# Layer change with pinned norms, projection matmuls grouped by weight part, and attention's low parts by accumulating DMA

## The chip, the cores and the metric

One core of one Trainium2 chip runs one launch. The metric is the device time of that launch in microseconds; less is better. A profile is one further execution, taken with the hardware profiler.

## The reference, cut to what matters

Two blocks run one after the other on 512 tokens of width 1024 in fp32.

```python
def first_block(x, ...):                      # one layer, 16 meta tokens ahead of x
    proj = rmsnorm(h, g) @ w_in               # u, q, k, v, g_ssm, g_att
    y_ssm = s5_mixer(u, ...)                  # complex scan
    q, k = rmsnorm(q, qg) * scale, rmsnorm(k, kg)
    o = diff_attention(q, k, v, lam, slopes)  # 4 heads, two softmaxes each
    h = h + mixed @ w_o
    h = h + conv_glu_ffn(rmsnorm(h, g2), ...)

def second_block(x, ...):
    for l in range(2):
        proj = rms_norm(x, pre_norm_g[l]) @ w_in[l]   # a_*, b_*, c_*, d_*
        y = concat(conformer(a), hgrn2(b), ssd(c), mla(d)) @ w_out[l]
        x = x + rms_norm(y, post_norm_g[l])
```

The stretch between `@ w_out[0]` and the projections of layer 1 is the layer change: the norm of `y` needs all of `y`, and every projection of layer 1 needs the new `x`.

## The kernel before

**Matrix work.** Each fp32 operand is split into a high part (`xh`, `wh`, the value rounded by a copy to fp32r) and a low part (`xl`, `wl`, the value minus the high part), and each product is three matmuls a 128-row block: `wh·xh`, `wh·xl`, `wl·xh`. Activations lie feature by token in eight tiles `hT` (128x512); `xn` holds their eight pairs `xh`, `xl`.

**Weights.** `weights()` hands out tiles in one fixed order and has four fetched ahead. `_fetch` makes a pair of 128x1024 parts: a DMA of SP into `wr`, a copy of ACT into `wh` (L439), a copy of ACT of `-wh` into `wl` (L441), then a DMA issued by POOL that adds the same weights from memory into `wl` (L442). `wh` and `wl` have four buffers each, so a new pair's copies wait until TensorE has used up the pair four back.

**Buffers.** PSUM banks come from rings: `pj` has three, `sA` and `sB` two each, `so` one. SBUF work tiles ("units") are reused first in, first out.

**Order.** A scheduler of the framework sets each engine's order from the program's order and its own plan. `tc.high_priority` moves an instruction up, `tc.keep_in_program_order` (called `pin` in the diff) fixes it to its place among the pinned ones and its neighbours. Side work (attention, the conv, scans) runs as generators: each `pump()` in a projection takes one step (up to the next `yield`) of each of them.

**Attention.** `qk_norm` normalises one tile of q or k. `k_parts` makes, for each half of the 128 partitions, a tile `ks` with the high part on one half (ACT, L1032) and the low part on the other (POOL subtraction, L1033). `q_parts` makes two tiles `qq` of high parts on both halves (ACT, L1044, L1045) and one `ql` of low parts (POOL subtraction, L1046). `attention_head` uses them in the scores (L1174, L1175).

**Second block.** `fm` is a projection with features on partitions (one weight pair, 24 matmuls of 512 columns); `tm` is one with tokens on partitions: two weight pairs, two banks `p`, 96 matmuls of 256 columns (L1480 to L1482), first all 48 of one bank, then all 48 of the other. `b_f` and `b_q` feed the hgrn branch: `zr` scales them (DVE, L1603), `hgrn_decay` takes the sigmoids (ACT, L1632, L1633) and the decay (DVE, L1646, a scan at L1651), and its scores are at L345. The projection after them, `tm` of mla's keys and ssd's steps, is called kvm below; the next is `d_cq`. Six `tm` run in a layer, in two rows of three; ACT copies each bank out (L2249).

**Layer change.** `out2(n, w, hs)` is output tile n of `@ w_out[0]` for a half `hs` of the tokens (24 matmuls, L2335 to L2337), the copy to `os[n]` and the addition of its squares into `st` (`ns_add`, ACT L528 and DVE L529). Tiles 0 to 4 run whole, 5 to 7 by halves `ha`, `hb`. `ns_finish(st, half)` is the norm: a matmul that sums the squares (L537) and two ACT operations (`rsqrt`, L498, L499). `add` multiplies by it (DVE, L2351), adds into `hT` (L2353; every third on POOL), splits into `xh`, `xl` (ACT L487, DVE L488) and adds the squares of the new `hT` into `self.st`. `lead(half)` is the first three projections of layer 1 (`b_f0`, `b_f1`, `b_q0`) for a half, 72 matmuls (L2366, L2368, L2369) into two `pj` banks and `so`.

Of the kernel before, what the change touches and what calls it, by code (L numbers as in the profile page):

```python
# [312 lines left out]
class Build:  # L313
# [172 lines left out]
    def split_scale(self, src, scale, xh, xl):  # L486
        self.nc.scalar.activation(out=xh, in_=src, func=AF.Copy, scale=scale)  # L487
        self.nc.vector.scalar_tensor_tensor(out=xl, in0=src, scalar=scale, in1=xh.bitcast(F32), op0=ALU.mult, op1=ALU.subtract)  # L488

# [5 lines left out]
    def rsqrt(self, p, out, eps):  # L495
        nc = self.nc
        with self.tc.issue_after(self.lnexp):
            nc.scalar.activation(out=out, in_=p, func=AF.Ln, bias=eps)  # L498
            nc.scalar.activation(out=out, in_=out, func=AF.Exp, scale=-0.5)  # L499
# [60 lines left out]
    def split_g(self, xn, n, x, g, hs):  # L560
        xh, xl = xn[n]
        self.split_scale(x, g[:, n:n + 1], xh[:, hs], xl[:, hs])
# [897 lines left out]
    def fm(self, l, nm, i):  # L1460
        w = self.weights(("in2", (l, nm, i)))
        p = self.pj()
        self.mm3(p, w[0], w[1], 0, 128, 8, self.xn, slice(0, S), mid=True)
        return p

    def tm(self, l, nm, N=256):
        mm = self.nc.tensor.matmul
        ws = [self.weights(("in2", (l, nm, i))) for i in range(2)]
        for b in range(2):
            p = self.pj()  # L1470
            for u in range(2):
                if u:
                    self.pump()
                o = p[:, u * 256:u * 256 + N]
                sl = slice((b * 2 + u) * 128, (b * 2 + u) * 128 + 128)
                for k in range(8):
                    c = slice((k % 4) * 256, (k % 4) * 256 + N)
                    h, lo = ws[k // 4][0][:, c], ws[k // 4][1][:, c]
                    xh, xl = self.xn[k]
                    mm(out=o, lhsT=xh[:, sl], rhs=h, start=k == 0, stop=False)  # L1480
                    mm(out=o, lhsT=xh[:, sl], rhs=lo, start=False, stop=False)  # L1481
                    mm(out=o, lhsT=xl[:, sl], rhs=h, start=False, stop=k == 7)  # L1482
            yield b, p
# [731 lines left out]
    def layer(self, l):  # L2215
# [37 lines left out]
        q0 = zs.pop()  # L2253
        kf = []
# [5 lines left out]
        q1 = self.zr(self.fm(l, "b_q", 1))  # L2260
# [66 lines left out]
        def out2(n, w, hs):  # L2327
# [20 lines left out]
        def add(hs, r):  # L2348
            for n in range(8):
                o = os[n][:, hs]  # L2350
                V.tensor_tensor(out=o, in0=o, in1=r[:, hs], op=ALU.mult)  # L2351
                E = G if n % 3 == 0 else V
                E.tensor_tensor(out=x[n][:, hs], in0=x[n][:, hs], in1=o, op=ALU.add)  # L2353
                self.split_g(self.xn, n, x[n][:, hs], self.v("preg1"), hs)
# [3 lines left out]
        def lead(hs, wl):  # L2358
            mm = nc.tensor.matmul
            for a in range(2):  # L2360
                for k in range(8):
                    xh, xl = self.xn[k]
                    c = slice(k * 128, k * 128 + 128)
                    for w, p in zip(wl, self.lead):
                        if a == 0:
                            mm(out=p[:, hs], lhsT=w[0][:, c], rhs=xh[:, hs], start=k == 0, stop=False)  # L2366
                        else:
                            mm(out=p[:, hs], lhsT=w[0][:, c], rhs=xl[:, hs], start=False, stop=False)  # L2368
                            mm(out=p[:, hs], lhsT=w[1][:, c], rhs=xh[:, hs], start=False, stop=k == 7)  # L2369
# [122 lines left out]
```

## Time and profile before

| what | value |
| --- | --- |
| median of 3 runs | 1374.3 us (1372.24 to 1375.38) |
| profiled execution | 1374.76 us, span 1373.0 us |
| TensorE (PE) busy | 1329.0 us, 97% of the span |
| VectorE (DVE), ScalarE (ACT), GpSimd (POOL) busy | 787.3, 780.8, 449.1 us |
| granted TensorE clock, mean | 0.988 |

The span is the profile's first to last instruction; the execution's own time is 1.76 us longer. With TensorE at 97%, the 44 us in which it stands idle and the stretches with a lower granted clock are where time can be had without fewer matmuls, and the table does not say where they lie. The rows below do.

### The profile page before, as it was taken

How to read it: one execution, taken by the hardware profiler on the slowest of the kernel's cores; microseconds unless marked ns; L12 is line 12 of the kernel's file. 1: busy time of each engine (PE TensorE's matmuls, PEld its weight loads, DVE VectorE, ACT ScalarE, POOL GpSimd, SP SyncE). 2: the span in 40 equal slices, each digit the busy share in tenths (PEclk: the TensorE clock that was granted, in tenths of full speed). 3: DMA queues.
4: the chain of work that ended last, by engine and by line, in shares of the span. 5: the costliest groups of instructions: out<-in, count | busy, mean ns of one | idle time of the engine just before them, and what ended most of it. 6: DMA issues, size and time to landing. Idle time of an engine off the chain costs nothing.

```text
span 1373.0 us, 22963 instructions
## 1 busy us (share of the span) xinstructions
PE 1329.0 (97%) x8778; PEld 1193.8 (87%) x8778; DVE 787.3 (57%) x1951; ACT 780.8 (57%) x1218; POOL 449.1 (33%) x557
## 2 busy tenths in 40 slices
PE   8999999999999999999999999899999789899998
PEld 8988899999999988998898889789988788789986
DVE  8989775423524322332233385998732785998623
ACT  7556564654555444444444766765566666764653
POOL 4557632113332211222123443532212344522210
PEclk9999999999999999999999999999999889999999
DMA  8944566598888888888887966994477367894483
GB/s 281 239 96 108 120 128 139 123 222 184 187 194 185 186 187 188 187 189 185 197 175 150 227 132 148 192 191 88 99 164 191 90 133 167 178 202 92 94 182 92
DMA packets 76861, 223.49 MB, mean 163 GB/s; under 512 B 11216, under 2 KB 21968, under 8 KB 76752
## 3 DMA queue, kind: packets, MB, share of 16 engines
q0 software_dynamic: 32256, 106.53, 46.7%
q1 hardware_dynamic: 43488, 113.80, 25.4%
q10 hardware_dynamic: 1008, 1.70, 0.4%
q8 instruction: 69, 1.13, 0.3%
q14 instruction: 40, 0.33, 0.1%
HBM read 209.33 MB, written 4.72 MB: 156 GB/s over the span
## 4 chain that ended last, share of the span: by engine, by line
PE 80%; DVE 14%; ACT 2%; issue 2%; DMA 1%; POOL 1%; SPq 0%; DVEq 0%; ACTq 0%; POOLq 0%
PE pj L466 18%; PE pj L467 18%; PE pj L468 18%; PE pj L1480 3%; PE pj L1482 3%; PE pj L1481 3%; PE sB L492 2%; DVE cc L1508 2%; PE sB L2152 1%; PE so L2180 1%; PE pj L2335 1%; PE pj L2336 1%; PE pj L2337 1%; DVE hx L1680 1%; PE so L1212 1%
## 5 line engine op out<-in xcount | busy, mean ns | idle before, releaser
L466 PE MATMUL pj<-xh,wh 128*128 128x512 f32 (+4 forms) x1700 | 556.5, 328 | 4.4 <-ACT mk L2120 2.4
L467 PE MATMUL pj<-xl,wh 128*128 128x512 f32 (+4 forms) x1700 | 553.1, 326 | 0.0
L468 PE MATMUL pj<-xh,wl 128*128 128x512 f32 (+4 forms) x1700 | 551.3, 325 | 0.0
L439 ACT ACTIVATE wh<-wr 128x1024 fp32r<-128x1024 f32 (+2 forms) x197 | 203.7, 1035 | 324.4 <-PE pj L467 294.1
L442 POOL DMA_DIRECT2D wl<-in_wst x192 | 169.3, 882 | 555.2 <-ACT wl L441 525.9
L466 PEld LDWEIGHTS pj<-xh,wh 128*128 128x128 f32 x1700 | 320.7, 189 | 33.0 <-ACT mk L2120 2.9
L467 PEld LDWEIGHTS pj<-xl,wh 128*128 128x128 f32 x1700 | 320.6, 189 | 27.0 <-issue 0.9
L468 PEld LDWEIGHTS pj<-xh,wl 128*128 128x128 f32 x1700 | 320.7, 189 | 26.3
L441 ACT ACTIVATE wl<-wh 128x1024 fp32r<-128x1024 f32 (+2 forms) x192 | 198.9, 1036 | 3.0 <-PE pj L468 0.2
L1481 PE MATMUL pj<-wl,xh 128*128 128x256 f32 x384 | 112.1, 292 | 5.5 <-DMA wl<-in_wst 5.5
L1480 PE MATMUL pj<-wh,xh 128*128 128x256 f32 x384 | 111.9, 292 | 2.1 <-DVE u L1603 2.1
L1482 PE MATMUL pj<-wh,xl 128*128 128x256 f32 x384 | 111.0, 289 | 0.0
L1481 PEld LDWEIGHTS pj<-wl,xh 128*128 128x128 f32 x384 | 74.1, 193 | 7.5 <-DMA wl<-in_wst 5.7
L1480 PEld LDWEIGHTS pj<-wh,xh 128*128 128x128 f32 x384 | 73.9, 192 | 3.5 <-ACT hk L1633 2.2
L1482 PEld LDWEIGHTS pj<-wh,xl 128*128 128x128 f32 x384 | 74.1, 193 | 1.6 <-issue 1.4
L1508 DVE SCALAR_TENSOR_TENSOR cc<-u,aw,cc 128x511 f32<-128x511 f32 (+20 forms) x84 | 67.0, 804 | 0.9
L1404 DVE TENSOR_TENSOR hT<-hT,pj 128x512 f32<-128x512 f32 x24 | 16.4, 687 | 88.4 <-PE pj L468 88.4
L1383 DVE TENSOR_TENSOR u<-pj,nsR 128x258 f32<-128x258 f32 (+1 forms) x44 | 18.6, 425 | 75.6 <-PE pj L468 68.3
L1389 DVE TENSOR_TENSOR u<-u,pj 128x512 f32<-128x512 f32 x22 | 15.1, 688 | 64.5 <-PE pj L468 60.2
L529 POOL TENSOR_TENSOR nsA<-nsA,u 128x514 f32<-128x514 f32 (+3 forms) x23 | 29.3, 1274 | 38.3 <-ACT u L528 28.8
L488 DVE SCALAR_TENSOR_TENSOR xl<-hT,vec,xh 128x256 fp32r<-128x256 f32 (+3 forms) x40 | 27.5, 703 | 18.7 <-ACT xh L487 18.7
L1515 POOL DMA_DIRECT2D ce<-u x28 | 24.6, 918 | 40.3 <-ACT mq L2113 10.8
(629 smaller groups left out, 2353.6 us busy)
## 6 DMA issues: line engine op xcount, KB each, us to landing
wr<-in_wst SPq DMA_DIRECT2D x183, 512.0 KB, 4.1
wl<-in_wst POOLq DMA_DIRECT2D x180, 512.0 KB, 6.1
hT<-in_xT SPq DMA_DIRECT2D x16, 264.0 KB, 5.8
wr<-in_wst SPq DMA_DIRECT2D x8, 384.0 KB, 3.1
wl<-in_wst POOLq DMA_DIRECT2D x8, 384.0 KB, 5.1
wr<-in_wst SPq DMA_DIRECT2D x6, 256.0 KB, 5.6
UD<-us SPq DMA_DIRECT2D x4, 264.0 KB, 9.2
U<-UD SPq DMA_DIRECT2D x16, 66.0 KB, 4.6
```

The source lines that it names most:

```text
L439: nc.scalar.activation(out=h[:, c], in_=raw[:, c], func=AF.Copy)
L441: nc.scalar.activation(out=l[:, c], in_=h.bitcast(F32)[:, c], func=AF.Copy, scale=-1.0)
L442: nc.gpsimd.dma_start(out=l[:, c], in_=self.ap["wst"][i, :, c], accum_op=ALU.add)
L466: mm(out=out, lhsT=a, rhs=xh[:, sl], start=k == 0, stop=False)
L467: mm(out=out, lhsT=a, rhs=xl[:, sl], start=False, stop=False)
L468: mm(out=out, lhsT=b, rhs=xh[:, sl], start=False, stop=k == nk - 1)
L488: self.nc.vector.scalar_tensor_tensor(out=xl, in0=src, scalar=scale, in1=xh.bitcast(F32), op0=ALU.mult, op1=ALU.subtract)
L529: eng.tensor_tensor(out=st["A"][:, hs], in0=st["A"][:, hs], in1=s[:, hs], op=ALU.add)
L1480: mm(out=o, lhsT=xh[:, sl], rhs=h, start=k == 0, stop=False)
L1481: mm(out=o, lhsT=xh[:, sl], rhs=lo, start=False, stop=False)
L1482: mm(out=o, lhsT=xl[:, sl], rhs=h, start=False, stop=k == 7)
L1508: V.scalar_tensor_tensor(out=c[:, o:S], in0=th[:, :S - o], scalar=aw[:, i, 30 - o:31 - o], in1=c[:, o:S], op0=ALU.mult, op1=ALU.add)
```

## The change

There are four parts. (1) The low parts of k and q are made like those of the weights: ACT copies the negative into place, and a DMA issued by POOL adds the fp32 value. (2) Each attention head takes two more steps (two `yield`) before its first instruction. (3) `fm` and `tm` run the matmuls that need `wh` first, those with `wl` after them; `tm` has both banks open at once and goes weight pair by weight pair. (4) At the layer change the norm's matmul is put at a fixed place inside the following matrix work (`at`), the splits of the first half are pinned between the copies of `out2`, all additions into `hT` run on DVE, the squares come after all splits, the second `lead` runs output by output, and layer 1's `b_q1` comes earlier in the program.

```diff
-    def rsqrt(self, p, out, eps):
+    def rsqrt(self, p, out, eps, pin=None):
...
@@ k_parts
             nc.scalar.activation(out=t[a], in_=f[a], func=AF.Copy)
-            nc.gpsimd.tensor_tensor(out=t[b], in0=f[a], in1=t[a].bitcast(F32), op=ALU.subtract)
+            nc.scalar.activation(out=t[b], in_=f[a], func=AF.Copy, scale=-1.0)
+            nc.gpsimd.dma_start(out=t[b], in_=f[a], accum_op=ALU.add)
@@ q_parts
         lo = self.unit(F32R, "ql")
+        nc.scalar.activation(out=lo[:, :S], in_=f[:, NM:], func=AF.Copy, scale=-1.0)
+        nc.gpsimd.dma_start(out=lo[:, :S], in_=f[:, NM:], accum_op=ALU.add)
...
-            nc.gpsimd.tensor_tensor(out=lo[a, :S], in0=f[a, NM:], in1=t[a, :S].bitcast(F32), op=ALU.subtract)
@@ attention_head
             yield
+        yield
+        yield
@@ fm
-        self.mm3(p, w[0], w[1], 0, 128, 8, self.xn, slice(0, S), mid=True)
+        for k, (xh, xl) in enumerate(self.xn):
+            a = wh[:, k * 128:k * 128 + 128]
+            mm(out=p, lhsT=a, rhs=xh[:, :S], start=k == 0, stop=False)
+            mm(out=p, lhsT=a, rhs=xl[:, :S], start=False, stop=False)
+            if k == 5:
+                self.pump()
+        for k, (xh, xl) in enumerate(self.xn):
+            mm(out=p, lhsT=wl[:, k * 128:k * 128 + 128], rhs=xh[:, :S], start=False, stop=k == 7)
@@ tm
-        for b in range(2):
-            p = self.pj()
-            for u in range(2):
...
+        ps = [self.pj() for _ in range(2)]
+        for q in range(2):
+            for t in range(2):
+                for b, p in enumerate(ps):
+                    for u in range(2):
...
+                        for k in range(4):
+                            if t:
+                                mm(out=o, lhsT=xh[:, sl], rhs=ws[q][1][:, c], start=False, stop=q + u + k == 5)
+                            else:
+                                mm(out=o, lhsT=xh[:, sl], rhs=ws[q][0][:, c], start=q + u + k == 0, stop=False)
+                                mm(out=o, lhsT=xl[:, sl], rhs=ws[q][0][:, c], start=False, stop=False)
@@ layer
         q0 = zs.pop()
+        q1 = self.zr(self.fm(l, "b_q", 1)) if l else None
...
-        q1 = self.zr(self.fm(l, "b_q", 1))
+        if not l:
+            q1 = self.zr(self.fm(l, "b_q", 1))
@@ layer change: out2
             for q, k in enumerate(korder):
+                if q == 3 and at:
+                    at()
...
-            nc.scalar.activation(out=os[n][:, hs], in_=p, func=AF.Copy, scale=pg[:, n:n + 1])
-            self.ns_add(st, n, p, hs, V)
+            with self.tc.high_priority(offset=400 if hs.stop - hs.start < S else 0):
+                i = nc.scalar.activation(out=os[n][:, hs], in_=p, func=AF.Copy, scale=pg[:, n:n + 1])
+                if n > 5 and hs.start:
+                    pin(i)
+                self.ns_add(st, n, p, hs, V)
@@ layer change: lead
+            for k in range(8):
+                if k == 5 and at:
+                    at()
+                for i in range(3):
+                    m = part(0, k, i)
...
+            if at:
+                for a in (1, 2):
+                    for k in range(8):
+                        for i in range(3):
+                            part(a, k, i)
+            else:
+                for i in range(3):
+                    for a in (1, 2):
+                        for k in range(8):
+                            part(a, k, i)
+        def norm(hs):
+            def at():
+                p = self.sB()[:, :256]
+                pin(nc.tensor.matmul(out=p, lhsT=self.o1024, rhs=st["A"][:, hs], start=True, stop=True))
+                with self.tc.high_priority(offset=600):
+                    self.rsqrt(p, st["R"][:, hs], self.eps6, None)
+                add(hs, st["R"])
+            return at
@@ layer change: the calls
-        r = self.ns_finish(st, ha)
-        add(ha, r)
-        for n in range(5, 8):
-            out2(n, ws[n - 5], hb)
+        out2(5, ws[0], hb, norm(ha))
+        split(ha, range(4), pin)
+        out2(6, ws[1], hb)
+        split(ha, range(4, 8), pin)
+        out2(7, ws[2], hb)
...
-        lead(ha, ws)
-        r = self.ns_finish(st, hb)
-        add(hb, r)
+        lead(ha, ws, norm(hb))
+        split(hb, range(8))
+        square(ha)
+        square(hb)
```

**Place 1: ACT, the first half's splits.** Before, on ACT, the splits (L487, `xh`) of the first half stand in a row, each followed by the square of the same `hT` (L525, L528); the copy of the last `out2` tile (L2338, `po_10956`) comes after the first of them.

```order
L487 ACTIVATE xh_11159<-hT_4059,vec 128x256
L525 ACTIVATE nsA_11157<-hT_4059 128x256
L2338 ACTIVATE po_10956<-pj_11233,vec 128x256
L528 ACTIVATE u_11401<-pj_11233 128x256
L441 ACTIVATE wl_11406<-wh_11405 128x1024
L487 ACTIVATE xh_11165<-hT_4062,vec 128x256
L528 ACTIVATE u_11305<-hT_4062 128x256
L487 ACTIVATE xh_11161<-hT_4060,vec 128x256
```

In the change, four splits stand ahead of the copy of `out2` tile 6 (`po_10963`, L2366 in the new file), and the other four ahead of that of tile 7.

```order
L487 ACTIVATE xh_11167<-hT_4067,vec 128x256
L528 ACTIVATE nsA_11165<-hT_4067 128x256
L487 ACTIVATE xh_11169<-hT_4068,vec 128x256
L531 ACTIVATE u_11523<-hT_4068 128x256
L487 ACTIVATE xh_11171<-hT_4069,vec 128x256
L531 ACTIVATE u_11526<-hT_4069 128x256
L487 ACTIVATE xh_11173<-hT_4070,vec 128x256
L2366 ACTIVATE po_10963<-pj_11212,vec 128x256
L441 ACTIVATE wl_11160<-wh_11159 128x1024
L531 ACTIVATE u_11351<-pj_11212 128x256
L531 ACTIVATE u_11529<-hT_4070 128x256
L487 ACTIVATE xh_11175<-hT_4071,vec 128x256
```

The squares of the last two `out2` tiles (L531 from `pj_11212` and later `pj_11241`), which the second half's norm needs, have moved behind the splits of the first half.

**Place 2: PE, the start of kvm.** Before, on PE, kvm (L1480 to L1482; banks `pj_11778`, `pj_11837`) opens three banks with one matmul each, and its fourth matmul is the first with a low weight part, `wl_11413`.

```order
L468 MATMUL pj_11713<-xh_11173,wl_11406 128x512
L1480 MATMUL pj_11778<-wh_11412,xh_11159 128x256
L1480 MATMUL pj_11837<-wh_11412,xh_11159 128x256
L1480 MATMUL pj_11926<-wh_11707,xh_11159 128x256
L1481 MATMUL pj_11778<-wl_11413,xh_11159 128x256
L1482 MATMUL pj_11778<-wh_11412,xl_11160 128x256
```

In the change (banks `pj_11786`, `pj_11787`) this is where the first low weight part comes in; 32 matmuls with `wh_11398` stand ahead of it, the last three of them shown.

```order
L1498 MATMUL pj_11787<-wh_11398,xl_11172 128x256
L1497 MATMUL pj_11787<-wh_11398,xh_11173 128x256
L1498 MATMUL pj_11787<-wh_11398,xl_11174 128x256
L1495 MATMUL pj_11786<-wl_11399,xh_11167 128x256
L1495 MATMUL pj_11786<-wl_11399,xh_11169 128x256
```

The need for the low part moved 29 matmuls down, and the second bank's last matmul now stands 8 behind the first bank's, where it stood 48 behind it.

**Place 3: PE, the hgrn scores of layer 1.** Before, on PE, the scores (L345) stand inside `d_cq` (banks `pj_11926`, `pj_12079`), after 30 of its 96 matmuls besides the one that kvm's start shows.

```order
L1482 MATMUL pj_11926<-wh_11707,xl_11160 128x256
L1480 MATMUL pj_11926<-wh_11707,xh_11161 128x256
L1481 MATMUL pj_11926<-wl_11708,xh_11161 128x256
L1482 MATMUL pj_11926<-wh_11707,xl_11162 128x256
L1480 MATMUL pj_11926<-wh_11707,xh_11163 128x256
L345 MATMUL sB_11901<-u_11735,u_11736 128x128
```

In the change they stand after 75 of the 96 (banks `pj_11934`, `pj_11935`).

```order
L1497 MATMUL pj_11935<-wh_11773,xh_11181 128x256
L1498 MATMUL pj_11935<-wh_11773,xl_11182 128x256
L1497 MATMUL pj_11935<-wh_11773,xh_11175 128x256
L1498 MATMUL pj_11935<-wh_11773,xl_11176 128x256
L345 MATMUL sB_11909<-u_11765,u_11766 128x128
```

So 44 to 45 more matmuls of `d_cq` are issued ahead of the scores. In layer 0 the scores stand 11 matmuls earlier than before. Attention's first scores stand 48 PE rows later than before, its last output 147 rows later (row 1763). The transposes of that output end at row 1828, and the products that use it begin at row 1948.

## Rows read from the trace of the kernel before

**Rows 1.** Windows: busy us (instructions) by engine, granted TensorE clock, DMA share, GB/s.

```profile
40.00:80.00 40.00, 37.85 (x279) 35.69 (x278) 39.46 (x109) 23.93 (x42) 25.80 (x37) 0.96 0.83 197
...
800.00:840.00 40.00, 36.61 (x304) 35.96 (x304) 32.03 (x94) 23.16 (x42) 15.59 (x19) 0.96 0.63 136
...
880.00:920.00 40.00, 36.36 (x179) 28.34 (x179) 37.56 (x91) 28.26 (x49) 14.40 (x16) 0.91 0.95 191
...
1040.00:1080.00 40.00, 34.78 (x253) 33.01 (x252) 22.52 (x51) 26.60 (x57) 15.76 (x23) 0.91 0.57 131
1080.00:1120.00 40.00, 29.32 (x215) 27.92 (x213) 29.30 (x66) 26.27 (x41) 17.29 (x24) 0.91 0.48 113
```

**Rows 2.** Waits of PE: its line <- the releaser: us in all, times, longest.

```profile
PE sB L345 <- DVE u L1670: 5.6, 2, 3.7
...
PE sA L902 <- DVE u L909: 2.1, 1, 2.1
PE pj L1480 <- DVE u L1603: 2.1, 1, 2.1
...
PE sA L946 <- DVE ST L929: 1.0, 1, 1.0
```

**Rows 3.** Timeline of PE: start us, us, instruction, idle before and its releaser.

```profile
1051.77 0.29 PE L2336 MATMUL pj<-xl,wh 128*128 128x256 f32 x1
...
1054.72 0.59 PE L537 MATMUL sB<-nsA,o 128*128 128x256 f32 x2
...
1061.46 0.50 PE L2366 MATMUL pj<-xh,wh 128*128 128x256 f32 x2 [1.43 <-ACT xh L487]
...
1065.88 1.19 PE L537 MATMUL sB<-nsA,o 128*128 128x256 f32 x2 [3.79 <-DVE nsA L529]
...
1100.61 0.58 PE L1481 MATMUL pj<-wl,xh 128*128 128x256 f32 x1 [5.49 <-DMA wl<-in_wst]
```

**Rows 4.** Timeline of ACT at the layer change and in layer 1's start.

```profile
1060.92 0.49 ACT L487 ACTIVATE xh<-hT,vec 128x256 fp32r<-128x256 f32 x1
...
1067.42 0.50 ACT L487 ACTIVATE xh<-hT,vec 128x256 fp32r<-128x256 f32 x1
...
1088.47 2.96 ACT L439 ACTIVATE wh<-wr 128x1024 fp32r<-128x1024 f32 x3 [1.66 <-PE pj L2368]
...
1092.74 0.63 ACT L1632 ACTIVATE hf<-u 128x512 f32<-128x512 f32 x1
...
1093.80 1.04 ACT L441 ACTIVATE wl<-wh 128x1024 fp32r<-128x1024 f32 x1
...
1111.69 0.72 ACT L2249 ACTIVATE u<-pj,s 128x196 f32<-128x196 f32 x2
...
1120.01 0.71 ACT L2249 ACTIVATE u<-pj,s 128x196 f32<-128x196 f32 x2
```

**Rows 5.** Timeline of DVE, the same stretch.

```profile
1051.93 0.42 DVE L529 TENSOR_TENSOR nsA<-nsA,u 128x256 f32<-128x256 f32 x1 [2.41 <-ACT u L528]
...
1058.51 3.85 DVE L2351 TENSOR_TENSOR po<-po,nsR 128x256 f32<-128x256 f32 x8 [2.50 <-ACT nsR L499]
...
1101.21 0.69 DVE L1646 TENSOR_TENSOR hf<-hf,u 128x512 f32<-128x512 f32 x1 [3.10 <-ACT hf L1644]
```

**Rows 6.** Lines of POOL, by form: busy us, mean ns of one, idle before.

```profile
L442 POOL DMA_DIRECT2D wl<-in_wst x192 | 169.3, 882 | 555.2 <-ACT wl L441 525.9 <-issue 8.2 <-PE pj L1482 7.3
...
L1033 POOL TENSOR_TENSOR ks<-qk,ks 64x528 fp32r<-64x528 f32 x8 | 11.1, 1389 | 0.6
L1046 POOL TENSOR_TENSOR ql<-qk,qq 64x512 fp32r<-64x512 f32 x8 | 10.5, 1312 | 1.5 <-ACT qq L1044 1.2
```

**Rows 7.** Timeline of DVE and of POOL in block 1.

```profile
61.03 2.67 DVE L673 TENSOR_TENSOR u<-CT,s_W 128x16 f32<-128x16 f32 x1
...
62.07 1.58 POOL L1046 TENSOR_TENSOR ql<-qk,qq 64x512 fp32r<-64x512 f32 x1
```

**Rows 8.** DMA issues: count, KB each, median us from issue to landing.

```profile
ce<-u POOLq DMA_DIRECT2D x4, 243.5 KB, 7.3
```

More of the change, by code (lines that the diff above doesn't have):

```diff
@@ L486, in split_scale @@
     def split_scale(self, src, scale, xh, xl):
-        self.nc.scalar.activation(out=xh, in_=src, func=AF.Copy, scale=scale)
+        i = self.nc.scalar.activation(out=xh, in_=src, func=AF.Copy, scale=scale)
         self.nc.vector.scalar_tensor_tensor(out=xl, in0=src, scalar=scale, in1=xh.bitcast(F32), op0=ALU.mult, op1=ALU.subtract)
+        return i
     def transposes(self, p, src, n=4, kk=128):
@@ L492, in transposes @@
             self.nc.tensor.transpose(p[:, j * 128:j * 128 + 128], src(j), self.ident[:kk, :kk])
-    def rsqrt(self, p, out, eps):
+    def rsqrt(self, p, out, eps, pin=None):
         nc = self.nc
         with self.tc.issue_after(self.lnexp):
-            nc.scalar.activation(out=out, in_=p, func=AF.Ln, bias=eps)
-            nc.scalar.activation(out=out, in_=out, func=AF.Exp, scale=-0.5)
+            for i in (nc.scalar.activation(out=out, in_=p, func=AF.Ln, bias=eps),
+                      nc.scalar.activation(out=out, in_=out, func=AF.Exp, scale=-0.5)):
+                if pin:
+                    pin(i)
     def rsq(self, ss, scale, eps, w, add=None):
@@ L1460, in fm @@
     def fm(self, l, nm, i):
-        w = self.weights(("in2", (l, nm, i)))
+        mm = self.nc.tensor.matmul
+        wh, wl = self.weights(("in2", (l, nm, i)))
         p = self.pj()
-        self.mm3(p, w[0], w[1], 0, 128, 8, self.xn, slice(0, S), mid=True)
+        for k, (xh, xl) in enumerate(self.xn):
[6 more added lines that the diff above has]
+            mm(out=p, lhsT=wl[:, k * 128:k * 128 + 128], rhs=xh[:, :S], start=False, stop=k == 7)
         return p
@@ L1468, in tm @@
         ws = [self.weights(("in2", (l, nm, i))) for i in range(2)]
-        for b in range(2):
-            p = self.pj()
-            for u in range(2):
[L1472 to L1483, printed above, removed]
+        ps = [self.pj() for _ in range(2)]
[3 more added lines that the diff above has]
+                    for u in range(2):
+                        o = p[:, u * 256:u * 256 + N]
+                        sl = slice((b * 2 + u) * 128, (b * 2 + u) * 128 + 128)
+                        for k in range(4):
+                            c = slice(k * 256, k * 256 + N)
+                            xh, xl = self.xn[q * 4 + k]
+                            if t:
[3 more added lines that the diff above has]
+                                mm(out=o, lhsT=xl[:, sl], rhs=ws[q][0][:, c], start=False, stop=False)
+                    if q and t:
+                        yield b, p
+                    elif q + t == 0 and b or q + t == 1 and not b:
+                        self.pump()
     @staticmethod
@@ L2325, in layer, with out2 @@
         pjs = [None] * 8
-        def out2(n, w, hs):
+        pin = self.tc.keep_in_program_order
+        def out2(n, w, hs, at=None):
             if hs.start == 0:
@@ L2348, in add @@
         def add(hs, r):
[L2349 to L2354, printed above, removed]
+            with self.tc.high_priority(offset=400):
+                for n in range(8):
+                    o = os[n][:, hs]
+                    V.tensor_tensor(out=o, in0=o, in1=r[:, hs], op=ALU.mult)
+                    V.tensor_tensor(out=x[n][:, hs], in0=x[n][:, hs], in1=o, op=ALU.add)
@@ L2355, in add, with split, square, lead @@
+        def split(hs, ns, keep=lambda i: i):
+            for n in ns:
+                with self.tc.high_priority(offset=400):
+                    keep(self.split_g(self.xn, n, x[n][:, hs], self.v("preg1"), hs))
+        def square(hs):
             for n in range(8):
                 self.ns_add(self.st, n, x[n][:, hs], hs, V if n % 2 else G)
-        def lead(hs, wl):
+        def lead(hs, wl, at=None):
             mm = nc.tensor.matmul
[L2360 to L2369, printed above, removed]
+            def part(a, k, i):
+                xh, xl = self.xn[k]
+                return mm(out=self.lead[i][:, hs], lhsT=wl[i][a // 2][:, k * 128:k * 128 + 128], rhs=(xl if a == 1 else xh)[:, hs],
+                          start=a == 0 and k == 0, stop=a == 2 and k == 7)
+            for k in range(8):
[3 more added lines that the diff above has]
+                    m = part(0, k, i)
+                    if k == 5 and at:
+                        pin(m)
+            if at:
[8 more added lines that the diff above has]
+                            part(a, k, i)
```

7 lines of the change are left out of this document (5 added, 2 removed).

## The prediction

> **What bounds the kernel now.** I read first the share of busy time, then the windows, then the waits of PE. TensorE is at 97% and the matmuls stay the same (the norm's are moved, not added), so only its idle time and its lower clock can be won. The windows [rows 1] show where these lie: in 1040 to 1120 us, the layer change and the start of layer 1, PE is busy 34.78 and 29.32 of 40 us, 15.9 us idle, at a granted clock of 0.91 in both. 800 to 840 (layer 0's hgrn stage) has 3.39 us idle, 880 to 920 has 3.64, and 40 to 80 (attention's start) 2.15. The lost clock is 40 us times one minus the clock: 3.6 + 3.6 us at the layer change, 1.6 in attention's window; 0.91 is a mixture of stretches at 2.4 and at 1.2 GHz.
>
> The waits name what is late. At the layer change and behind it five hold nearly all of the idle time: 1.43 for the first split (L487), 3.79 for the second half's norm (L537), 5.49 for kvm's low weight part [rows 3], 2.1 at kvm for L1603, and 3.7, the longest of L345's two, at the hgrn scores [rows 2]. In attention two waits of 2.1 (L902) and 1.0 (L946) are for DVE [rows 2].
>
> **Attention: the low parts.** Gone are 8 subtractions of k and 8 of q on POOL, 11.1 + 10.5 = 21.6 us [rows 6]. In come 12 DMA issues at 0.882 us, as the weights' accumulating DMAs take to issue: 10.6 us. POOL saves 11 us, worth nothing by itself, since POOL does not bound. ACT gets 12 more copies at about 0.63, what a 512-column ACT operation takes [rows 4]: 7.6 us, with ACT busy 60% in that window [rows 1]. They are hidden except where one stands ahead of a copy that PE waits for; three times 0.63, 2 us, is my lower bound.
>
> What can be won is DVE's time. At 61.03 a DVE operation of only 16 columns took 2.67 us and ended at 63.70, 0.05 after a subtraction of q on POOL (62.07 to 63.65) [rows 7]. L909, for which PE waits 2.1, comes behind it on DVE. The Trainium skill, page "SBUF — State Buffer", section "SBUF: two separate sides", says that a DVE operation with two SBUF inputs and a GpSimd operation that reads SBUF shut each other out for the whole instruction; this row agrees. By that rule both waits would go with the subtractions, and the term would be 3.1.
>
> From the rows, the two waits are 3.1 us, and 1.6 us of clock are lost in that window, 4.7 in all. Other POOL work stays beside the same DVE chain (the long operation began before the subtraction did), so I take 3.0. Bounds: 2 lost, 4.7 won.
>
> **Attention: two steps later.** A matmul of 256 columns takes 0.118 at full clock: 25 of them from 1051.77 to 1054.72 [rows 3]. One of 512 counted as two, the first scores' 48 rows are some 11 us. An accumulating DMA of a like size lands in 7.3 us [rows 8], issue 0.9: covered. At the end the last head's output comes 147 rows later, and the products that use it stand 120 rows behind its last transposes, some 28 us: covered too. If that cover were gone, the last head's few us would stand bare before the mixer's product.
>
> **Layer change, first half.** The norm's matmul stands 23 matmuls earlier in the same work: 1054.72 - 23 x 0.118 = 1052.0. Its squares are ready at 1051.93 + 0.42 = 1052.35 [rows 3, 5], so PE waits 0.35. Its two ACT operations have priority over weight copies now, and I estimate DVE's multiplication at about 1054 where it was 1058.51. Eight of these take 3.85 [rows 5], an addition follows, and the first split comes at about 1058.45 where it was 1060.92 [rows 4], before PE has finished `out2`. So the 1.43 at lead's first matmul goes.
>
> **Second half.** Here the pins cost. The squares of `out2` tiles 6 and 7, which this norm sums, stand behind four and eight splits of the first half (place 1). Before, the first and the last of eight splits started 6.5 us apart (1060.92, 1067.42), with one copy, its square and one weight copy between [rows 4]. With the same, and one copy and square more, the last split starts at 1058.45 + 6.5 + 0.6 = 1065.5, the last square ends at about 1066.2, DVE adds it, and the norm's matmul comes at about 1066.75, later than the 1065.88 of before [rows 3]. But 15 lead matmuls stand ahead of it where 3 did, 12 x 0.118 = 1.4. Net, the first lead ends some 0.4 earlier: the 1.43 saved at its start has gone into a wait of about 3 that stays.
>
> **kvm.** This is the larger gain. Its `wl` is late because its copies on ACT wait for lead to use up a buffer: `wh` at 1088.47 (released by PE's L2368), `wl` at 1093.80 to 1094.84 [rows 4], landed when PE goes on at 1100.61 [rows 3], 5.8 after the copy. Lead's last 48 matmuls now run output by output, so the first pair is free 32 matmuls before their end: 1088.47 - 32 x 0.118 = 84.7. The `wl` copy then ends by about 87, and lands by 93. PE comes to kvm at about 1092 (1100.61 less 5.5, 2.1 and the first three matmuls) and needs `wl` only behind 32 matmuls, 3.8 later. The 5.5 goes. The 2.1 too: the third bank, which waited for L1603, is not opened there (place 2). So 7.6 us are gone at this place.
>
> **What is late next** is the hgrn chain of layer 1. Two of the three weight copies ahead of its sigmoid on ACT (2.96 us together) come earlier, so the sigmoid comes at about 1089.5 where it was 1092.74 [rows 4], L1646 on DVE at 1097.9 where it was 1101.21 [rows 5]. Between it and the scores DVE has the same work, and some that now comes earlier: I take 2.7 earlier for the scores. By then PE has 45 more matmuls of `d_cq` behind it (place 3), 5.3 us. 2.7 + 5.3 = 8.0 gained at this point, with a wait still there, of about 4.4. But what used to stand behind the scores and hid two small chains (ssd's and mla's norm) is now ahead of them: L1913 stands 16 rows after the scores. I take 3 back, the ssd chain's and the norm's few DVE operations. Net 5.0. Bounds: 1.5 (about half of the chain's 2.7) and 9.0 (nothing given back, and 1 of the 7.2 of clock).
>
> **Layer 0 and the grouped matmuls.** The scores stand 11 matmuls earlier here, and their wait is 5.6 - 3.7 = 1.9 [rows 2]. I take 1.0 won. Bounds -3 and +3, near the 3.39 and 3.64 of idle time in its two windows [rows 1]. Grouping by weight part changes no matmul's length; a `b_q1` earlier in layer 1's program stands among lead's matmuls before and now.
>
> **Sum.** 3.0 + 5.0 + 1.0 = 9.0. From the profiled execution, 1374.76 (span 1373.0 and 1.76 around it), that is 1365.8; this execution lies 0.46 over the median of the runs, so the forecast as a median is 1365.3. All lower bounds: 2 - 1.5 + 3 = 3.5 slower. All upper: 4.7 + 9 + 3 = 16.7 faster, 1357.6.
>
> **Rivals.** What a measurement can't tell from no change is 0.2%, 2.75 us.
>
> *All of it goes.* The 15.9 us of idle time and 7.2 of clock at the layer change: 1374.3 - 23.1 = 1351.2. For it: the waits follow from one another, and the clock falls with them. Against it: the second norm's chain through ACT and DVE is no shorter. Chance 0.08.
>
> *No change.* The hgrn chain sets the scores' time whatever PE does ahead of them, and the 45 matmuls put ahead only move the wait: 1.5 won there, nothing elsewhere, 1372.8. For it: PE waits for that chain in both layers already. Against: matmuls done ahead need not be done behind. Chance 0.17.
>
> *Slower: the banks of `tm`.* Its two banks now end 8 matmuls apart, and the next `tm` wants its second bank 16 matmuls (1.9 us) after its first. Before, ACT copied kvm's two out 8.3 us apart, 1111.69 and 1120.01 [rows 4], with other work between. There are four such successions a layer, eight in all. At 2.2 us each they cost 17.6: 1365.3 + 17.6 = 1382.9; slower than can be mistaken is reached at (9.0 + 2.75) / 8 = 1.5 each. Against it: both copies become ready together now, and at `d_cq` 41 matmuls stand on the first bank. Chance 0.09.
>
> *Accumulating DMAs late.* If each of four heads waits 4 us for its low parts, half a landing of 7.3, 16 us: 1381. Against it: the cover of 11 us, and weight DMAs that take 0.88 to issue [rows 6]. The Trainium skill, same page, in its box on "DVE blocks DMA", says that while DVE runs an operation that uses both ports, GpSimd can't write the descriptors of a DMA that it issues, which then looks blocked; that speaks against this change where DVE is fullest, 39.46 of 40 us [rows 1]. No row here shows such a stall at an issue. Chance 0.03.
>
> **How the numbers follow.** The forecast has 0.63. With each term half way to its bounds the gain is 2.8 to 12.9, its own range 1361 to 1372. The range takes in the no-change case, the tails of the forecast, and the near part of the two extremes: 1354 to 1376 leaves out 1351 (0.08), and most of 1381 and 1383 (0.10). Faster: 0.60 of the forecast's, 0.08, and 0.05 of the no-change case, 0.73. Same: 0.03 + 0.12 + 0.01 = 0.16. Slower: 0.11.
>
> **What would show it.** In the profile after: no wait at kvm for `wl`; a wait of about 4 at layer 1's L345, ending 2.7 us earlier on the clock, and by the 4 more that attention and layer 0 win; a wait of about 3 before the second norm; L902's and L946's waits gone or halved; idle time behind the layer change down from 15.9 to about 10. Wrong would be waits of `tm`'s matmuls for ACT's copies, of scores for `ks` or `ql`, or a later stage of layer 1 that takes the gain back.

## The result and the profile after

The changed kernel takes 1383.2 us (median of 4 runs, 1380.56 to 1384.96) against 1374.68 (4 runs, 1372.24 to 1375.38): a ratio of 1.0062, 95% interval 1.0044 to 1.0079. It is slower by 8.5 us, where 9.0 faster was forecast, and lies outside the range. The profiled execution is the fastest of the four (1380.56, span 1378.8), so its rows account for 5.8 us of the 8.5. Line numbers are higher in the changed kernels: L902 is L905 there, L946 is L949, L1670 is L1689, and the matmuls of `tm` stand at L1495 to L1498.

The windows of the changed kernel, with the columns of [rows 1]:

```profile
40.00:80.00 40.00, 37.99 (x300) 36.69 (x300) 39.48 (x115) 25.87 (x45) 23.19 (x38) 1.00 0.87 207
80.00:120.00 40.00, 35.19 (x242) 31.17 (x241) 24.80 (x60) 21.33 (x46) 21.20 (x33) 0.96 0.55 117
...
880.00:920.00 40.00, 31.32 (x160) 25.78 (x159) 29.03 (x66) 25.58 (x42) 13.86 (x15) 0.87 0.88 182
1040.00:1080.00 40.00, 35.76 (x229) 32.78 (x228) 19.18 (x48) 26.69 (x51) 9.56 (x13) 0.92 0.74 169
1080.00:1120.00 40.00, 39.23 (x304) 37.90 (x304) 29.96 (x67) 31.17 (x56) 17.54 (x26) 0.99 0.64 151
1120.00:1160.00 40.00, 35.12 (x248) 32.39 (x247) 33.64 (x97) 23.74 (x42) 15.45 (x19) 0.91 0.62 130
1160.00:1200.00 40.00, 34.34 (x208) 28.71 (x207) 32.47 (x64) 25.90 (x41) 20.23 (x23) 0.91 0.83 163
```

The layer change comes out much as forecast. That 1080 to 1120 has 0.8 us idle where [rows 1] have 10.7 says too much, since all of it comes 7.75 us later here and the wait at the scores has left that window. The 80 us of [rows 1], moved by 7.75, have 9.8 us idle where 15.9 were and about 10 was forecast, with the clock at 0.94 in place of 0.91:

```profile
1047.75:1127.75 80.00, 70.17 (x523) 67.12 (x523) 55.42 (x131) 55.94 (x106) 29.84 (x42) 0.94 0.63 141
```

But 880 to 920 has 8.7 us idle at a clock of 0.87 where there were 3.6 at 0.91, and 80 to 120 has 4.8 where there were 2.2. The waits of PE, as in [rows 2], name it:

```profile
PE sB L345 <- DVE hD L1754: 12.8, 2, 7.9
PE sB L345 <- DVE u L1689: 8.5, 2, 4.8
PE sB L2423 <- DVE nsA L532: 3.1, 2, 2.8
PE sB L1018 <- DVE s L1210: 2.6, 1, 2.6
...
PE sB L1018 <- ACT u L1011: 1.4, 1, 1.4
...
PE sA L905 <- DVE Zi L911: 1.1, 1, 1.1
PE pj L2399 <- ACT u L531: 1.1, 1, 1.1
```

The waits of the forecast are there: 2.8 before the second norm (about 3 forecast), 4.8 at layer 1's first scores (4.4 forecast), no wait at kvm. Not forecast is the 1.1 of L2399: in the first `lead`, the bank of one projection is still read by the square of an `out2` tile (L531), which place 1 showed behind the splits. The first line is new as well: the hgrn scores of the widest level (also L345) wait 7.9 us in layer 0 and 4.9 in layer 1 for `hD` of DVE's L1754, the copy that empties their `sB` bank. Followed back in layer 0, on DVE:

```profile
875.87 0.68 DVE L2305 SCALAR_TENSOR_TENSOR u<-u,pj 128x512 f32<-128x512 f32 x1
...
880.05 0.16 DVE L519 SCALAR_TENSOR_TENSOR s<-s,s 128x8 f32<-128x8 f32 x1
890.78 0.55 DVE L1518 TENSOR_SCALAR cc<-u,aw,vec 128x512 f32<-128x512 f32 x1 [10.57 <-POOL u L2306]
891.25 0.77 DVE L1754 COPY_PREDICATED hD<-msk,sB 128x256 f32<-128x256 int32 x2
```

and on POOL:

```profile
880.80 0.86 POOL L1534 DMA_DIRECT2D ce<-u  x1 [2.28 <-DMA ce<-u]
887.70 0.86 POOL L1538 DMA_DIRECT2D ce<-ce  x1 [6.04 <-DMA ce<-u]
888.24 1.22 POOL L442 DMA_DIRECT2D wl<-in_wst  x1
888.80 1.95 POOL L2306 TENSOR_TENSOR u<-u,nsR 128x512 f32<-128x512 f32 x1
```

Read from the bottom: L2306, the product from which the conv of the second channel tile starts, stands on POOL behind L1538, which adds up the first tile's conv and waits 6.0 us for a DMA. Its own input, L2305 on DVE, was done at 876.55, 12 us before it began. DVE's L1518 waits 10.57 us for the product, L1754 stands behind it on DVE, and PE's scores wait for L1754. Before, the product stood ahead of that accumulation:

```profile
879.29 1.61 POOL L2285 TENSOR_TENSOR u<-u,nsR 128x512 f32<-128x512 f32 x1
883.96 0.88 POOL L1519 DMA_DIRECT2D ce<-ce  x1 [3.06 <-DMA ce<-u]
```

For the runs below the span is cut at two places that each trace shows: the start of the first hgrn scores of layer 0 (block 1 and attention ahead of it), and the start of the last `wh·xh` matmul of `out2` (layer 0 up to its end). The rest is the layer change and layer 1.

| kernel (its profiled execution) | to the scores | layer 0 | rest |
| --- | --- | --- | --- |
| before | 809.6 | 249.9 | 313.5 |
| changed | 813.2 | 254.1 | 311.5 |
| e1 tm_two_pumps | 813.0 | 244.3 | 307.9 |
| e2 fm_tm_before | 811.7 | 247.8 | 305.6 |
| e3 attention_before | 809.5 | 253.8 | 305.7 |
| e4 layer_change_before | 813.7 | 254.8 | 310.2 |
| e5 attn_before | 810.4 | 246.2 | 304.8 |
| e6 steps_alone | 819.1 | 246.0 | 305.5 |
| e7 dma_alone | 811.3 | 246.5 | 307.3 |
| e8 hold_tile | 817.9 | 246.4 | 306.8 |
| e9 other_tile | 823.9 | 244.2 | 304.3 |
| e10 layer_change_alone | 808.9 | 250.6 | 307.2 |
| e11 grouping_alone | 809.1 | 246.2 | 314.5 |
| e12 product_on_dve | 812.8 | 245.8 | 311.6 |
| e13 other_tile_dma | 809.3 | 249.2 | 307.4 |
| e14 one_step | 818.3 | 245.3 | 309.6 |

There is one profile of each kernel. Kernels whose code is the same in a part still differ there, by up to 2.0 us to the scores, 5.0 in layer 0 and 5.3 in the rest, so a smaller difference in this table shows nothing alone; whole times are compared by the ratios. In layer 0 the kernels with three steps in `tm` (see e1) and the product on POOL stand clear of that: 253.8 to 254.8 for changed, e3 and e4, against 244.2 to 249.2 with two steps and grouped matmuls, and 247.8 to 250.6 with `tm` as before.

### The profile page after: what moved, and what is told of

It reads as the page before. It is cut to its first block, busy times and chain, and to the rows that moved or that the text cites. A ratio compares the mean times of both kernels' runs of the same rounds, so it can differ in the third digit from the quotient of the medians.

```text
span 1378.8 us, 22990 instructions
## 1 busy us (share of the span) xinstructions
PE 1330.1 (96%) x8778; PEld 1196.1 (87%) x8778; DVE 776.2 (56%) x1957; ACT 787.0 (57%) x1230; POOL 430.7 (31%) x547
## 4 chain that ended last, share of the span: by engine, by line
PE 76%; DVE 7%; DMA 4%; issue 3%; ACT 3%; POOL 2%; SPq 0%; DVEq 0%; POOLq 0%; ACTq 0%
PE pj L466 14%; PE pj L468 14%; PE pj L467 14%; PE pj L1473 3%; DMA ce<-u 3%; PE pj L1474 3%; PE pj L1495 3%; PE pj L1478 3%; PE pj L1497 3%; PE pj L1498 3%; PE sB L493 2%; PE sB L2171 1%; PE so L2199 1%; PE pj L2363 1%; PE pj L2364 1%
## 5 line engine op out<-in xcount | busy, mean ns | idle before, releaser
L466 PE MATMUL pj<-xh,wh 128*128 128x512 f32 (+4 forms) x1468 | 462.0, 315 | 3.7 <-DVE u L2128 1.6
L467 PE MATMUL pj<-xl,wh 128*128 128x512 f32 (+4 forms) x1468 | 459.5, 313 | 0.0
L468 PE MATMUL pj<-xh,wl 128*128 128x512 f32 (+4 forms) x1468 | 459.5, 313 | 0.0
L466 PEld LDWEIGHTS pj<-xh,wh 128*128 128x128 f32 x1468 | 276.8, 189 | 23.0 <-DVE u L2128 2.0
L468 PEld LDWEIGHTS pj<-xh,wl 128*128 128x128 f32 x1468 | 276.8, 189 | 17.9 <-issue 0.2
L467 PEld LDWEIGHTS pj<-xl,wh 128*128 128x128 f32 x1468 | 276.8, 189 | 17.0 <-issue 0.2
L1498 PE MATMUL pj<-wh,xl 128*128 128x256 f32 x384 | 95.7, 285 | 0.0
L1473 PE MATMUL pj<-xh,wh 128*128 128x512 f32 x232 | 92.9, 401 | 0.0
L1474 PE MATMUL pj<-xl,wh 128*128 128x512 f32 x232 | 92.3, 398 | 0.0
L1498 PEld LDWEIGHTS pj<-wh,xl 128*128 128x128 f32 x384 | 73.4, 191 | 1.4 <-issue 1.2
L1527 DVE SCALAR_TENSOR_TENSOR cc<-u,aw,cc 128x511 f32<-128x511 f32 (+17 forms) x84 | 64.4, 773 | 0.6
L1478 PE MATMUL pj<-xh,wl 128*128 128x512 f32 x232 | 61.5, 399 | 0.0
L1495 PE MATMUL pj<-wl,xh 128*128 128x256 f32 x384 | 56.0, 291 | 0.8 <-DMA wl<-in_wst 0.8
```

What stands on the lines that cost most here:

```text
L466: mm(out=out, lhsT=a, rhs=xh[:, sl], start=k == 0, stop=False)
L467: mm(out=out, lhsT=a, rhs=xl[:, sl], start=False, stop=False)
L468: mm(out=out, lhsT=b, rhs=xh[:, sl], start=False, stop=k == nk - 1)
L1473: mm(out=p, lhsT=a, rhs=xh[:, :S], start=k == 0, stop=False)
L1474: mm(out=p, lhsT=a, rhs=xl[:, :S], start=False, stop=False)
L1478: mm(out=p, lhsT=wl[:, k * 128:k * 128 + 128], rhs=xh[:, :S], start=False, stop=k == 7)
```

## The experiments

**e1, two steps of side work in `tm`.** The changed `tm` gives the generators three steps inside its matmuls; the one of before gave two. The two of e1 stand behind 32 and 48 of the 96 matmuls, the three of the change behind 32, 40 and 64, the two of before behind 24 and 72.

```diff
-                    elif q + t == 0 and b or q + t == 1 and not b:
+                    elif q == 0 and b:
                         self.pump()
```

> The changed kernel with one edit: tm gives the side work two steps inside its matmuls, as before the change, and not three. Theory A (the conv's side work runs a step ahead, so POOL's accumulation of the conv, which waits for a DMA, stands ahead of the product that the second conv tile starts from, DVE stands behind that, and PE's scores behind DVE): the two waits of L345 for hD, 12.8 us in all, fall under 1 us; of the 6.8 us of smaller waits that stood there before the change some 5 come back; with 1.5 of clock the time is 1383.2 - 9 = about 1374 to 1377. Rival B (the grouping by weight part, with both banks open, is what costs): 1381 to 1385, and the hD waits stay above 8 us.

Measured: 1366.94, 0.994 of before (0.9918 to 0.9961). Better than forecast by theory A; rival B falls. POOL's product is ahead again:

```profile
880.43 1.52 POOL L2306 TENSOR_TENSOR u<-u,nsR 128x512 f32<-128x512 f32 x1
883.47 0.87 POOL L1538 DMA_DIRECT2D ce<-ce  x1 [1.52 <-DMA ce<-u]
```

The waits for `hD` that were 12.8 are gone, layer 0 takes 9.8 us less and the rest 3.6, though layer 1's first scores now wait 6.8 (for L1898 on DVE). The windows of layer 0, in the changed kernel and in e1, show that 6.9 of the 9.8 are idle time of PE and 2.9 busy time, at a clock of 0.99 in place of 0.97:

```profile
813.20:1067.30 254.10, 244.62 (x1586) 216.58 (x1587) 166.80 (x435) 153.65 (x256) 70.84 (x84) 0.97 0.68 146
813.00:1057.30 244.30, 241.72 (x1579) 213.53 (x1580) 171.95 (x435) 153.39 (x257) 73.24 (x84) 0.99 0.70 152
```

One `if` thus turned 0.6% slower into 0.6% faster.

One part of theory A does not hold: the conv itself does not run a step ahead. It is started behind the three `tm` of its row, four `pump()` stand between its start and the product in either kernel, and L1538 belongs to its eighth step, so in the program's order the product is ahead of L1538 in all three kernels. What the third step moves is the side work that was started earlier: the first hgrn scores of the widest level come at 850.1 in the changed kernel, at 860.1 before and at 860.7 in e1. It is the framework's scheduler that set L1538 ahead of the product in the changed kernel; why its plan did so stays open.

**e2, `fm` and `tm` as before.** Both functions are put back whole.

```diff
-        ps = [self.pj() for _ in range(2)]
-        for q in range(2):
...
+        for b in range(2):
+            p = self.pj()
+            for u in range(2):
...
```

> The changed kernel with fm and tm as before. Theory A: the hD waits fall under 1 us, as in the run with two steps, but kvm's wait for its low weight part comes back in part (2 to 5.5 us): 1376 to 1381, slower than the run with two steps by 2 to 5. Rival B (grouping costs): as fast as the run with two steps, or faster.

Measured: 1369.39, 0.9963 (0.995 to 0.9977). L345's waits for `hD` fall to 0.7, though another matmul of the hgrn branch (L1738) waits 3.1 for `hD` in layer 1, and kvm's wait for `wl` comes back at 3.5 us (it was 5.49 in [rows 3]). These are theory A's signs; the time is 7 us under its range. Grouping with two steps is faster than none by 0.23%, but their intervals overlap, so it is e1 that rules out rival B, and not this run. Here the two steps stand at the places of before, and the long waits of L345 are gone as in e1, which speaks for the number of steps and not their places; no run varies the two apart.

**e3, attention as before.** POOL's subtractions back, no further steps for the heads.

```diff
-            nc.scalar.activation(out=t[b], in_=f[a], func=AF.Copy, scale=-1.0)
-            nc.gpsimd.dma_start(out=t[b], in_=f[a], accum_op=ALU.add)
+            nc.gpsimd.tensor_tensor(out=t[b], in0=f[a], in1=t[a].bitcast(F32), op=ALU.subtract)
...
-        yield
-        yield
```

> The changed kernel with POOL's subtractions for the low parts and without the two steps more, as before. Theory C (attention lost 3 us because tiles that an accumulating DMA still reads are reused, so DVE waits for the DMA): 1383.2 - 3 = about 1380, with the out-projection's first tile some 3 us earlier. Rival D (attention's part is no loss by itself): 1382 to 1385.

Measured: 1371.71, 0.9982 (0.9969 to 0.9994). The time is 8 us under theory C's. The scores of layer 0 come 3.7 earlier, as it said of attention; the rest is shorter too, by 5.8, which the theory does not explain. With three steps kept, layer 0's wait for `hD` stays at 7.0, but layer 1's is 1.6 where the changed kernel has 4.9.

**e4, layer change as before,** with the place of `b_q1`.

```diff
-        out2(5, ws[0], hb, norm(ha))
-        split(ha, range(4), pin)
...
+        r = self.ns_finish(st, ha)
+        add(ha, r)
...
```

> The changed kernel with the layer change as before (out2, add, lead, the place of b_q1). Theory E (the layer change with grouped matmuls won about 7 us up to the first scores of layer 1, which a later wait hides): 1386 to 1391. Rival F (grouping alone removed kvm's wait, the pins nothing): 1382 to 1385.

Measured: 1378.62, 1.0025 (1.001 to 1.004). Both theories fall: without the new layer change the kernel is faster than with it, by 0.37%. Both profiled executions took 1380.56 us, so their rows can't say where. In e4's, layer 1's wait for `hD` is 1.0, where the changed kernel has 4.9, with others of 2.9 (L2149), 1.9 (`wl`) and 1.5 (L493) there: beside the third step, what the layer change wins is waited for again. The third step alone does not do it, since e3 has it too and a rest of 305.7.

**e5 to e8, attention taken apart,** each with two steps in `tm`: e5 has e3's edit, e6 only the subtractions back (the heads' steps kept), e7 only the steps undone, and e8 gives the tile that the DMA reads back one step later:

```diff
         p = self.k_parts(f) if dm is self.km else self.q_parts(f)
-        self.free(f)
         yield
+        self.free(f)
```

> The run with two steps in tm, and attention's low parts and heads as before. Theory C (attention lost its time because work tiles that an accumulating DMA or a DMA behind it still reads come up for reuse, and ACT, DVE and SP stand in their queues for it): layer 0's first hgrn scores 3 to 4 us earlier than 813.0, and 1366.9 - 4 = 1362 to 1363. Rival D (attention's part costs nothing by itself): 1366 to 1368, the scores at 812 or later.

Measured: 1362.67, 0.9917 (0.9896 to 0.9938), theory C's time, with the scores 2.6 earlier where it said 3 to 4. The fastest kernel of the study. Against e1 it is 0.23% faster, and the intervals overlap.

> The run with two steps in tm, with POOL's subtractions back but the heads' two further steps kept. Theory C1 (the DMAs are the cost): like attention as before, 1362 to 1364, with no wait of ACT's L810 near 10 us. Rival C2 (the two steps alone shift which tiles are reused, whatever makes the low parts): 1366 to 1368, that wait of 7 to 10 us still there.

Measured: 1371.81, 0.9988 (0.9976 to 1.0). C2, and worse than it said in time: the scores at 819.1, 8.7 later than in e5, while ACT's wait is 5.9 and not 7 to 10. Block 1's largest waits on PE:

```profile
60.95 0.72 PE L905 MATMUL sA<-U,V 128*128 128x132 f32 x4 [1.98 <-DVE s L867]
...
72.38 1.00 PE L905 MATMUL sA<-U,V 128*128 128x132 f32 x3 [4.75 <-DVE Zi L911]
```

With the DMAs (e1) these two are 0.90 and 1.10.

> The run with two steps in tm, with the low parts by accumulating DMA but the heads at their former steps. Theory C1: 1366 to 1369, with DVE's wait of 3.7 for the DMA of ql and ACT's of 9.7 for the DMA of ys, and more waits of scores for ks or ql. Rival C2: 1362 to 1364 without these waits.

Measured: 1365.0, 0.9939 (0.9921 to 0.9957). The time lies between the two ranges. ACT's wait is gone, as C2 said, but DVE waits for the DMA of `ql` at another place (L833, 6.2 and 3.6 us). The two waits for DVE (L905, L949) that the prediction was after are gone, but head 0's scores now wait for `ql`, as C1 said:

```profile
66.65 0.45 PE L1180 MATMUL sB<-ks,ql 64*128 64x256 f32 x1 [3.85 <-DMA ql<-qk]
```

3.1 won, 3.85 lost: the scores at 811.3, 0.9 later than in e5, which is within the spread.

> The run with two steps in tm, where the tile that the accumulating DMA reads is given back one step later. Theory C: the wait of 3.7 of DVE's L912 for the DMA of ql goes and with it some of ACT's 9.7: 1363 to 1365. Rival: the same waits come at another reader of another tile, 1366 to 1368.

Measured: 1372.62, 0.9989 (0.9978 to 1.0001). The rival or worse: holding one tile moves all that follow in the row of free tiles, and other waits appear (3.2 and 2.6 us in block 1).

**e9 and e13, another tile for CT.** The changed kernel's ACT has this row in attention; SP's queue issued that DMA only at 98.58:

```profile
103.19 0.31 ACT L810 ACTIVATE CT<-cta 128x128 f32<-128x128 f32 x1 [10.04 <-DMA YD<-ys]
```

Units are reused first in, first out, and the heads' two steps move the row so that the third quarter's `CT` gets `ys`, which a DMA has still to read. The wait, 5.0 to 10.9 us, is there in each of e1, e2, e4, e6, e8 and e12, and in none of the kernels without the two steps. e9 (from e6) and e13 (from e1) skip that tile:

```diff
+        if q == 2:
+            self.free_units.append(self.free_units.pop(0))
         CT = self.unit(F32, "CT")
```

> The run with the heads' two steps alone, where the third S5 quarter's tile CT skips the oldest free tile (the ys of the quarter before, which a DMA still has to read) and takes the next. Theory H (the two steps shift the row of free tiles by a few, so CT's copy on ACT stands in its queue for that DMA): ACT's wait of 5.9 for the DMA of ys goes, the first hgrn scores of layer 0 come at 811 to 815 and not at 819.1, time 1364 to 1368. Rival I (the steps cost through the order of the heads among S5's work): 1370 to 1373.

> The run with two steps in tm (low parts by DMA, heads two steps later, as in the change), where the third S5 quarter's CT skips the oldest free tile, ys, and takes the next. Theory H (this one reuse costs the waits at 104.8 and 110.6, 4.4 us, and the lower clock behind them, 0.91 in 80 to 120): ACT's wait of 9.7 goes, PE idles under 2 us in 80 to 120 where it was 4.45, the first hgrn scores come at 806 to 809 and not at 813.0; 1360 to 1363. Rival I (the order of the heads among S5's work costs it, and the wait only shows where): 1365 to 1368, scores at 811 or later.

Measured: e9 1371.12, 0.9965 (0.9951 to 0.9979); e13 1365.64, 0.9933 (0.9914 to 0.9951). ACT's wait is gone in both. In e13 PE's window of 80 to 120 goes from e1's

```profile
80.00:120.00 40.00, 35.55 (x232) 31.71 (x232) 24.74 (x59) 20.14 (x45) 19.99 (x33) 0.91 0.56 117
```

to

```profile
80.00:120.00 40.00, 39.69 (x278) 35.96 (x277) 29.49 (x73) 25.00 (x51) 25.31 (x38) 0.96 0.65 136
```

and the scores come 3.7 earlier (809.3). So this reuse cost what theory H said at its place; the whole time is rival I's and does not show it (0.9940 and 0.9933, intervals that overlap). Layer 0 takes 4.9 more than in e1 (second line of windows there), most of it busy time at a lower clock:

```profile
809.30:1058.50 249.20, 245.12 (x1578) 215.65 (x1579) 172.79 (x435) 153.23 (x256) 72.26 (x83) 0.98 0.68 148
```

Whether the kernel or the one execution lowers the clock there is not shown. In e9 the reuse was not what cost: up to the scores PE idles 19.8 us with the other tile and 19.9 without (e6). The 4.8 by which e9's scores are later still are busy time at a lower clock, in the slowest of its seven executions (1374.33). The time is rival I's.

**e10, layer change alone; e11, grouping alone.** e10 has the edits of e2 and e3 on the changed kernel, e11 those of e1, e3 and e4.

> The kernel before with the layer change alone (fm, tm and attention as before). Theory E (it wins 6 to 8 us when no side work is shifted): 0.994 to 0.996 of before, 1366 to 1369. Rival F (only together with grouped matmuls): 0.998 to 1.001.

> The kernel before with fm and tm grouped by weight part and two steps in tm (attention and layer change as before). Theory: kvm's wait for its low weight part falls from 5.5 to under 2, and no wait for hD above 1: 0.995 to 0.998 of before, 1368 to 1371. Rival B (two banks open at once cost bank waits): 1.000 or more, with waits of tm's matmuls for ACT's copies of 4 us or more in all.

Measured: e10 1368.4, 0.9947 (0.9927 to 0.9967), theory E. e11 1372.35, 0.9979 (0.997 to 0.9988): the ratio that was said, but waits for `wl` of 3.4 in all, 2.4 of them at kvm, where under 2 were said, and one of 2.2 for `hD` (L1746). Together they make e5: 0.53% and 0.21% against 0.83%.

**e12, the product on DVE,** with the three steps kept.

```diff
-            G.tensor_tensor(out=th[:, :S], in0=th[:, :S], in1=self.r[:, :S], op=ALU.mult)
+            V.tensor_tensor(out=th[:, :S], in0=th[:, :S], in1=self.r[:, :S], op=ALU.mult)
```

> The changed kernel, three steps in tm kept, with the product that the conv starts from on DVE and not on POOL. Theory A: DVE's wait for that product goes, L345's waits for hD fall from 12.8 to under 3 us, time 1372 to 1377. Rival J (the third step moves the scores ahead of their chain, whatever POOL does): L345 keeps 8 us or more of such waits, 1380 to 1384.

Measured: 1374.35, 0.9994 (0.9981 to 1.0008). Theory A: no wait for `hD` is left among the larger ones, and layer 0 takes 8.3 less. The rest is as long as in the changed kernel (311.6), though layer 1's 4.9 for `hD` are gone. In place of them L466 waits 3.2 and L2171 1.7 for ACT there; the wait of the first scores, 5.3, was 4.8 already. Of each line the longest is in layer 1:

```profile
PE sB L345 <- DVE u L1689: 9.0, 2, 5.3
PE pj L466 <- ACT mq L2119: 5.2, 2, 3.2
```

**e14, one further step for the heads,** two steps in `tm`.

```diff
         yield
-        yield
         q, k, vt = qs[h], ks[h], self.vts[h]
```

> The run with two steps in tm and low parts by DMA, but the heads one step later in place of two; CT then takes another tile than ys. Theory H: no wait of ACT for the DMA of ys, and a wait of scores for ql under the 3.9 of no further step: 1360 to 1364. Rival I (each step costs some 4 us): 1365 to 1368.

Measured: 1376.61, 1.0011 (0.9999 to 1.0023), worse than none and than two. Both theories fall: there are new waits of 3.8 at a norm and 3.4 at scores, and behind the second DVE stands 3.4 for the DMA `ks<-qk`. No run shows why one step is so much worse than none or two.

## Why the prediction was wrong

**The step that failed** is in the part on layer 0 and the grouped matmuls: "Grouping by weight part changes no matmul's length" was taken to mean that the new `tm` costs nothing. The matmuls are indeed no longer for it; but `tm` also decides when the side work goes on, and the changed one gives it a third step. The prediction counted matmuls and banks and never the steps, and its three places are orders of ACT and PE; POOL's, in which L1538 stands ahead of the product, is not among them. e1, which takes the third step out, is worth 1.2% (1.0062 to 0.9940), 16 us in medians, more than the whole sum of 9.0. e12 shows the place from the other side: with the three steps kept and the product off POOL, 8.3 us of layer 0 come back.

That e1 measures 8.0 faster, near the 9.0 of the sum, is luck: its parts are 3.4 lost to the scores, 5.6 won in layer 0 and 5.6 in the rest, where 3.0, 1.0 and 5.0 won were forecast.

**Attention, 3.0 won.** The sign was wrong, the reasons half right. The operation of 16 columns [rows 7] takes 2.65 to 2.67 us in all kernels with attention as before (before, e3, e5, e10, e11) and 0.17 in e7, without the subtractions and with the heads at their former steps:

```profile
56.29 0.17 DVE L676 TENSOR_TENSOR u<-CT,s_W 128x16 f32<-128x16 f32 x1
```

The two waits for DVE go with them (e7), and with the heads late the DMAs win 6.1 us to the scores (e6 to e1). The cover of the two steps was needed: without them `ql` is 3.85 late, so the rival "accumulating DMAs late" is right there, for one head. What was priced at nothing, the steps themselves, costs 8.7 alone (e6 against e5). With both, attention loses 2.6 to the scores (e1 against e5); in whole times it is 0.23%, not clear of the intervals. Without the reuse of `ys` the scores come 3.7 earlier than in e1, level with e5's (e13); why the steps cost 8.7 beside the subtractions (e6, e9), and why one step beside the DMAs costs more than two (e14), stays open.

`ql`'s DMA of the second head took 8.5 us to land, from 88.12; POOL issued it in 0.87 us, like the other three, and DVE stood idle in the last 3.7 of these 8.5, waiting for it. The box "DVE blocks DMA" in the Trainium skill, page "SBUF — State Buffer", says that GpSimd can't write a DMA's descriptors while DVE runs a two-port operation. That can't have held this DMA in those 3.7 us, and for the time before them no run here tells.

**Layer change, 5.0 won.** Right in nearly all its steps: first norm matmul's wait 0.33 (0.35 forecast), the second's 2.8 (3), kvm's gone, 4.8 at the scores (4.4). Counted from the start of the last `wh·xh` matmul of `out2` (1059.5 before, 1067.3 now), the first split, the first sigmoid, L1646 and the scores come within 0.7 us of the times forecast. Missed was the 1.1 that `lead` waits for a bank (L2399). Alone the layer change measured 0.53%, 6.6 us in medians (e10). In the changed kernel a later stage of layer 1, the 4.9 for `hD`, takes much of it back, the last of the signs that the prediction named: the rest is 2.0 shorter than before.

**Layer 0, 1.0 won:** it lost 4.2; with two steps it wins 5.6 (e1).

**The rival that came nearest in time,** the banks of `tm`, had the wrong mechanism: among the changed kernel's waits of 0.4 us or more there is none of `tm`'s matmuls for ACT's copies. In e5, where the rest is out of the way, one of the eight successions does wait, 4.0 us (as in e6, e8 and e9, 4.0 to 5.1), since ACT's copy stands behind an operation that waits for DVE:

```profile
1106.91 0.63 ACT L1682 ACTIVATE u<-u 128x512 f32<-128x512 f32 x1 [3.65 <-DVE u L1680]
1107.44 0.72 ACT L2264 ACTIVATE u<-pj,s 128x196 f32<-128x196 f32 x2
```

## What to carry to other kernels

Where side work is stepped by calls inside a matmul loop, count the steps of a rewritten loop against the old one, and read the new order of every engine's queue, not only of those that were to change: here one POOL instruction that waits for a DMA, set ahead of a product, held up POOL, DVE and TensorE. Price a move of side work by the buffers too: a first-in-first-out pool hands a tile that a DMA still reads to whoever comes at that turn. Of a change with several parts, run each alone: here layer change and grouping with two steps make 0.9917 together, and the other edits turned that into 1.0062.

## What the hardware showed that was not expected

How long an accumulating DMA of 256 KB takes to land goes with the weight accumulations of POOL that have not landed when it is issued. Nine kernels make `ql` by such DMAs, four each. With no weight accumulation in flight they landed in 3.3 to 4.1 us (9 DMAs), with one in 3.3 to 7.9 (21), with two in 8.0 to 8.8 (6: the second head's in changed, e1, e2, e4, e12 and e13). That the weight accumulations delay it is argued from this, not shown: no run changes them alone.
